# A two-block transformer kernel: first outputs in two parts, LRU off Pool, a narrower causal mask, keys stored once and a new order of tiles in attention

## The chip, the cores and the metric

The kernel runs on one core of a Trainium2 chip. The metric is the device time of one execution in microseconds. The engines are TensorE (PE: matmuls, with PEld for the loading of their weights), VectorE (DVE), ScalarE (ACT), GpSimd (POOL) and SyncE (SP, which issues DMAs). Every DMA is issued from a queue of SP or POOL.

## The reference

The reference computes one token sequence of 1024 tokens and width 1024. Cut to what the change touches:

```python
# first block: gating (4 heads), a state-space branch, cross attention to 256 memory tokens
y = concatenate([y_a * silu(g_a), y_b * silu(g_b), y_x * silu(g_x)], -1)
x = layer_norm(DN_ALPHA * x + y @ w_out, ln_g, ln_b)
# second block, on x normalised again: an LRU branch (conv of 4 taps, gates, a scan over tokens) ...
a = exp(-c * softplus(lam) * r);  h[t] = a * h[t-1] + sqrt(1 - a*a) * (i * x)[t]
# ... and a causal attention with differential heads (two softmaxes of 64-wide heads, subtracted),
# queries and keys RMS-normalised and rotated; then an output product, a mixer over memory, and a MoE
s = where(causal, q @ k.T, -inf);  o = (softmax(s1) - lam * softmax(s2)) @ v
```

All of it is computed in f32 accuracy: an operand is split into a rounded high part and a low part (`split`: ACT copies the high part, DVE subtracts to get the low part), and one product is three matmuls (high x high, low x high, high x low; `mm3`, L174 to L176).

## The kernel before, in words

The program is written as stages that follow each other, and a scheduler fixes a static order of instructions for each engine. In the profile the stages lie so: the first block from 0 to about 338 us, `ln1` (the first block's output product and its layer norm) to 461, `lru` to 705, `attention` to 1460, then the output product, the mixer and the MoE to the end.

**First block to ln1.** The gated outputs of the first block are stored to DRAM tiles `yb[h]` by `store_y` (L527), from SP. In `block1` a lane `left()` handles gating heads 2 and 3, another lane, `attend()`, heads 0 and 1; after a point in the list `LWAT` each a piece of `w_out` is loaded (`self.wo`). `ln1` (L957) works through 8 tiles of 128 tokens: it loads a tile of `yb` (`load`: L1595, split into `yh` and `yl`), multiplies it by `w_out` (`po`, 48 matmuls of 512 columns), adds `x`, normalises (DVE, with POOL for the reciprocal square root of L179 and for the last addition into `x1t`), normalises once more into `xnt`, and transposes (`ptr`, L949) into `xnh` and `xnl`, the operand of everything in the second block.

**LRU.** `lru` (L1036) works through 8 chunks of 128 channels over all 1024 tokens. Each has two projections (`pj`, 48 matmuls of 512 columns each), a convolution on DVE (`xc`), gates (`pg`; `tr` and `ti` on ACT), elementwise work of 128x1024 each on DVE and ACT (`tau`, `ex`, `rn`, `sq`, `q`), and a scan (L1122). In 7 of the 8 chunks two products, `sq*rn` and `ti*sq`, run on POOL. Side work on the memory tokens (`mem2`: `kn`, `kv`, `mh`) lies between.

**Attention.** There are 4 pairs of heads p, each with 16 units (one query tile of 128 tokens, one head half). A unit is: `unit_qk` (L1455), scores `sc` as `qs` x `kh` and `qs` x `kl` in pieces of 256 to 512 key columns, plus one matmul for the causal mask (`ma` x `mb`, L1481, always 256 columns); `unit_mix`, the softmax on DVE and ACT (`st`, `e`); `unit_tr` (L1511), transposes `pt` of the weights, split into `wth` and `wtl`; `unit_pv` (L1523, L1524), `po`; `unit_o`. Between these, generators called `fillers` supply matmuls that do not hang on the softmax: key tiles (project, normalise and rotate in `norm_rope`, transpose), value tiles, query tiles and gate tiles (`pg`, 512 columns). The key side is stored twice in each transposed tile: 4 transposes (L1248) of 128 columns for a key tile of 128 tokens. `need` runs fillers until a query tile exists. After the last unit of a pair come the 8 key and value tiles of the next pair, a key tile and a value tile in turn.

Of the kernel before, what the change touches and what calls it, by code (L numbers as in the profile page):

```python
# [11 lines left out]
F32 = mybir.dt.float32  # L12
# [114 lines left out]
LWAT = (5, 8, 11, 14)  # L127


class Model:  # L130
# [321 lines left out]
    def block1(self):  # L452
# [3 lines left out]
        self.yb = [D.tile([4, 128, 8, 128], F32, name=f"yb{h}") for h in range(2)]  # L456
# [67 lines left out]
        def store_y(k, t0, y, n):  # L524

            i = t0 % 4
            nc.sync.dma_start(out=self.yb[t0 // 4][i:i + n, :, k, :].rearrange("i p t -> p i t"),  # L527
                              in_=y.rearrange("p (i t) -> p i t", i=n))
# [289 lines left out]
        def gating(hp, side, wload, vps, pm_):  # L818
# [25 lines left out]
            def spatial(h, vh, vl):  # L844
                for hh in range(2):
# [17 lines left out]
                    store_y(hd, 4 * h, y, 4)  # L863
                    yield
# [33 lines left out]
        def left():  # L898
# [6 lines left out]
            self.wo = []  # L905
            for n, r in enumerate(gating(1, None, lambda a, b: weights(a, b, "d"), lambda c: (PB, "pb", 2),
                                         (PJ, "pj", 2))):
                yield r
                if n in LWAT:
                    k = len(self.wo)  # L910
                    self.wo.append(self.load_w(LW, A["w_out"][0, k], [128, 2, 512], f"wo0{k}", (W, "wd", 1)))
# [44 lines left out]

    def ln1(self):  # L957
# [4 lines left out]
        with self.pool("lnw1") as LW, self.pool("lny", side="right") as NW, self.pool("ln", side="right") as N, self.pool("lnps", bufs=2, space=PSUM) as PO, \  # L962
                self.pool("lnpt", bufs=2, space=PSUM) as PT:
# [7 lines left out]
            ring = (NW, "raw", 4)  # L971

            def load(i):
                yh = NW.tile([128, 8, 128], F32R, name="yh", tag="yh", bufs=2)
                yl = NW.tile([128, 8, 128], F32R, name="yl", tag="yl", bufs=2)
                eng = nc.gpsimd if i < 2 else nc.sync
                self.load_split(self.yb[i // 4][i % 4], yh, yl, ring, eng)
                return yh, yl

            def load_x(i):  # L980
                xr = N.tile([128, 1024], F32, name="xr", tag="xr", bufs=2)
# [3 lines left out]
            nxt = [load(0), load(1)]  # L985
            nxx = [load_x(0), load_x(1)]
            wo = self.wo + [self.load_w(LW, A["w_out"][1, k], [128, 2, 512], f"wo1{k}", ring) for k in range(4)]
            for i in range(8):
                yh, yl = nxt.pop(0)
                xr = nxx.pop(0)  # L990
                ps = PO.tile([128, 2, 512], F32, name="po", tag="po")
                for n in range(2):
                    for k in range(8):
                        w = wo[4 * n + k // 2]
                        self.mm3(ps[:, n], (yh[:, k], yl[:, k]), (w[0][:, k % 2], w[1][:, k % 2]), k == 0, k == 7)
# [15 lines left out]
                if i < 6:  # L1011
                    nxx.append(load_x(i + 2))
# [8 lines left out]
                self.tt(x1, x1, lb, OP.add, nc.gpsimd)  # L1021
# [7 lines left out]
            finish()  # L1029
            finish()  # L1030
# [1444 lines left out]
```

## Time and profile before

| what | value |
|---|---|
| median of 3 runs | 2524.95 us (2524.49 to 2526.47) |
| the profiled execution: its time, its span | 2524.15 us, 2522.4 us |
| granted TensorE clock, mean | 0.981 |
| busy share of the span | PE 94%, PEld 78%, DVE 71%, ACT 49%, POOL 22% |
| PE busy in the stages: first block / ln1 / lru / attention / rest | 313.5 of 338 / 112.6 of 123 / 229.1 of 244 / 714.5 of 755 / 996.5 of 1062 us |

A profile row of a matmul shows its duration through the pipeline (0.28 us for 256 columns); what it costs on a full PE is the distance from its start to the start of the next. Time that an engine sat idle stands in brackets behind a row of the timeline, with what ended it.

### The profile page before, as it was taken

To read this page: it belongs to the slowest core of one execution; us is meant where nothing else is said; L and a number is where in the kernel's file an instruction comes from. 1 tells how busy PE (TensorE), PEld (TensorE's weight loads), DVE (VectorE), ACT (ScalarE), POOL (GpSimd) and SP (SyncE) were. 2 spreads that over 40 slices of the span, in tenths; PEclk is the share of its full clock that TensorE was granted. 3 is DMA by queue.
4 is the path that set the end of the run, shared out by engine and by line. 5 is a ranking of instruction groups with operands and counts; after the bars stand their busy time and mean duration, and the time that the engine had idled before them with its cause. 6 is when DMAs were issued, how large, how long until landed. Compare 5 with 4: busy or idle time off the path is not lost. (4 is left out here: it accounts for less than half of the span.)

```text
span 2522.4 us, 34498 instructions
## 1 busy us (share of the span) xinstructions
PE 2366.1 (94%) x13016; PEld 1956.4 (78%) x13016; DVE 1786.7 (71%) x3206; ACT 1246.9 (49%) x1850; POOL 546.1 (22%) x377
## 2 busy tenths in 40 slices
PE   8999989989989999899999899999988999988887
PEld 6888868777888898798898778888876777666665
DVE  9667767686876666666666744336658999988887
ACT  5344532553655455455454522124435777766664
POOL 1011114112131021021121100000002333255552
PEclk9999999999999999999999999999988999999999
DMA  6321353322111111111111456532158998999995
GB/s 222 95 76 61 112 200 113 109 70 89 63 60 46 63 46 39 51 51 38 51 51 47 146 198 218 181 137 82 70 217 290 381 372 311 367 335 337 337 334 188
DMA packets 103833, 394.29 MB, mean 156 GB/s; under 512 B 14128, under 2 KB 33072, under 8 KB 79088
## 3 DMA queue, kind: packets, MB, share of 16 engines
q1 hardware_dynamic: 85008, 335.18, 37.6%
q0 software_dynamic: 18656, 56.88, 7.2%
q8 instruction: 104, 1.70, 0.3%
q14 instruction: 65, 0.53, 0.1%
HBM read 339.07 MB, written 61.31 MB: 159 GB/s over the span
## 5 line engine op out<-in xcount | busy, mean ns | idle before, releaser
L166 DVE TENSOR_TENSOR wl<-raw,wh 128x2048 fp32r<-128x2048 f32 (+2 forms) x310 | 580.8, 1887 | 118.3 <-ACT wh L154 118.0
L154 ACT ACTIVATE wh<-raw 128x2048 fp32r<-128x2048 f32 (+2 forms) x310 | 479.7, 1557 | 286.2 <-PE pj L175 83.4
L2238 POOL DMA_INDIRECT out<-y,lsti x32 | 175.2, 5475 | 331.4 <-DVE y L162 281.5
L175 PE MATMUL pg<-wl,xh 128*96 128x512 f32 x512 | 205.4, 401 | 30.2 <-DVE wl L166 30.0
L174 PE MATMUL pj<-wh,xnh 128*128 128x256 f32 x768 | 223.0, 290 | 10.8 <-ACT pc L154 6.0
L175 PE MATMUL pj<-wl,xnh 128*128 128x256 f32 x768 | 218.1, 284 | 0.0
L176 PE MATMUL pj<-wh,xnl 128*128 128x256 f32 x768 | 217.8, 284 | 0.0
L176 PE MATMUL pg<-wh,xl 128*96 128x512 f32 x512 | 201.6, 394 | 0.0
L174 PE MATMUL pg<-wh,xh 128*96 128x512 f32 x512 | 198.2, 395 | 1.0 <-ACT wh L154 1.0
L174 PEld LDWEIGHTS pj<-wh,xnh 128*128 128x128 f32 x768 | 146.0, 190 | 14.3 <-ACT pc L154 8.1
L175 PEld LDWEIGHTS pj<-wl,xnh 128*128 128x128 f32 x768 | 146.2, 190 | 0.0
L176 PEld LDWEIGHTS pj<-wh,xnl 128*128 128x128 f32 x768 | 145.9, 190 | 0.0
L175 PEld LDWEIGHTS pg<-wl,xh 128*96 128x96 f32 x512 | 82.8, 162 | 76.5 <-DVE wl L166 44.6
L179 POOL TENSOR_TENSOR ss<-ss,mhalf 128x4 f32<-128x4 f32 (+1 forms) x68 | 73.0, 1074 | 313.7 <-DVE ss L163 219.3
L154 ACT ACTIVATE e<-sc,st,ss 128x1024 f32<-128x1024 f32 (+7 forms) x128 | 105.7, 829 | 67.3 <-DVE st L158 50.4
L174 PEld LDWEIGHTS pg<-wh,xh 128*96 128x96 f32 x512 | 82.8, 162 | 37.2 <-ACT wh L154 1.4
L174 PE MATMUL pj<-xnh,wh 128*128 128x512 f32 x256 | 103.3, 404 | 5.6 <-ACT wh L154 5.6
L176 PEld LDWEIGHTS pg<-wh,xl 128*96 128x96 f32 x512 | 83.0, 162 | 32.7
L174 PE MATMUL pg<-xnh,wh 128*128 128x512 f32 x256 | 102.9, 402 | 0.0
L175 PE MATMUL pj<-xnl,wh 128*128 128x512 f32 x256 | 102.2, 399 | 0.0
L176 PE MATMUL pg<-xnh,wl 128*128 128x512 f32 x256 | 102.1, 399 | 0.0
L176 PE MATMUL pj<-xnh,wl 128*128 128x512 f32 x256 | 101.9, 399 | 0.0
(998 smaller groups left out, 6480.8 us busy)
## 6 DMA issues: line engine op xcount, KB each, us to landing
raw<-in_w_gu SPq DMA_DIRECT2D x128, 1024.0 KB, 7.3
raw<-in_w_dn SPq DMA_DIRECT2D x64, 1024.0 KB, 9.2
raw<-in_w_out SPq DMA_DIRECT2D x16, 512.0 KB, 4.7
ta<-tg POOLq DMA_DIRECT2D x32, 256.0 KB, 2.6
t<-ta SPq DMA_DIRECT2D x14, 512.0 KB, 4.6
raw<-in_w_ga SPq DMA_DIRECT2D x12, 512.0 KB, 3.8
raw<-in_w_v SPq DMA_DIRECT2D x12, 512.0 KB, 3.4
xraw<-in_xT SPq DMA_DIRECT2D x8, 512.0 KB, 7.6
```

The source lines that it names most:

```text
L154: return self.nc.scalar.activation(out=out, in_=in_, func=func, **kw)
L166: return (eng or self.nc.vector).tensor_tensor(out=out, in0=a, in1=b, op=op)
L174: mm(ps, l[0], r[0], start=start, stop=False)
L175: mm(ps, l[0], r[1], start=False, stop=False)
L176: mm(ps, l[1], r[0], start=False, stop=stop)
L179: self.nc.gpsimd.tensor_tensor(out=out, in0=in_, in1=self.mhalf[:, :w], op=OP.pow)
L2238: return nc.gpsimd.indirect_dma_start(out=self.out, out_offset=bass.IndirectOffsetOnAxis(ap=u["row"], axis=0), in_=u["y"], in_offset=None, ...
```

## The change

It has seven parts.

1. **First outputs in two parts.** `yb[h]` becomes two tensors, one of six columns `YA` (0, 1, 4 to 7) and one of columns 2 and 3. The six-column part of token tile 0 is loaded in `left()` by SP (`y_first`), and `ln1` multiplies it for tiles 0 and 1 ahead of columns 2 and 3. Three pieces of `w_out` are loaded ahead instead of four, the ring of raw buffers in `ln1` has 3 slots instead of 4, and `x` is loaded one tile ahead instead of two.
2. **Last norm's addition.** For token tiles 6 and 7 the addition into `x1t` moves from POOL to DVE.
3. **LRU's first product first.** The first half (512 tokens) of LRU's first projection is written into `ln1`, ahead of the transposes of the last token tile, and copied into `li0`.
4. **LRU off POOL.** `sq*rn` and `ti*sq` run on DVE in all chunks; a small memset moves too; the ring of gate weights "g" has one buffer instead of two.
5. **Mask.** `ma` and `mb` become bf16, and the mask matmul covers 64 columns instead of 256.
6. **Keys once.** `norm_rope` writes a key tile once, so 2 transposes a tile instead of 4; `kk` holds high and low key parts on two halves of the partitions, and `qs` the high and the low part of the queries. A score piece is still two matmuls of the same width.
7. **New order.** The key tiles of the next pair are fillers behind the last gate tiles of this pair; the value tiles of the next pair run within its first unit (`need(vals, p)`). For pair 0 all key tiles come ahead of all value tiles. `tg`, `ot` and `t` share the buffers of `nr`.

```diff
-LWAT = (5, 8, 11, 14)
+LWAT = {5: 0, 8: 2, 11: 3}
+YA = (0, 1, 4, 5, 6, 7)
...
+        self.yb = [[D.tile([4, 128, w, 128], F32, name=f"yb{h}{w}") for w in (6, 2)] for h in range(2)]
...
+                elif n > 8 and not self.y0 and ("gate", 1, 0) in self.made:
+                    self.y0 = self.y_first(YE, 0, (W, "wr", 2))
...
+    def y_first(self, P, i, ring):
+
+        hi = P.tile([128, 6, 128], F32R, name=f"ya{i}h")
+        lo = P.tile([128, 6, 128], F32R, name=f"ya{i}l")
+        return self.load_split(self.yb[i // 4][0][i % 4], hi, lo, ring)
...
-            ring = (NW, "raw", 4)
+            ring = (NW, "raw", 3)
...
+            for k in (4, 6, 7, 1, 5):
+                wo[k] = self.load_w(LW, A["w_out"][k // 4, k % 4], [128, 2, 512], f"wo{k // 4}{k % 4}", ring)
...
+            for i in range(2):
+                product(i, YA)
             for i in range(8):
...
+                product(i, (2, 3) if i < 2 else YA + (2, 3))
...
-                self.tt(x1, x1, lb, OP.add, nc.gpsimd)
+                self.tt(x1, x1, lb, OP.add, nc.vector if i > 5 else nc.gpsimd)
...
             finish()
+
+            ps = P0.tile([128, 512], F32, name="pj", tag="pj")
+            for k in range(8):
+                self.mm3(ps, (self.w0[0][:, k], self.w0[1][:, k]), self.xnc(k, 0), k == 0, k == 7)
+            self.li0 = w0.tile([128, 512], F32, name="li0")
+            self.act(self.li0, ps, AF.Copy)
             finish()
...
-                eng = nc.vector if c == 7 else nc.gpsimd
-                self.tt(sq, sq, rn, OP.mult, eng)
-                self.tt(ti, ti, sq, OP.mult, eng)
+                self.tt(sq, sq, rn, OP.mult)
+                self.tt(ti, ti, sq, OP.mult)
...
-            ma = T.tile([128, 128], F32R, name="ma")
-            mb = T.tile([128, 384], F32R, name="mb")
+            ma = T.tile([128, 128], BF, name="ma")
+            mb = T.tile([128, 64], BF, name="mb")
...
+                w = 1 if is_k else 2
+                d = T1.tile([128, 4, w, 64], F32, name="nr", tag="nr", bufs=3)
...
+                    for m in range(2):
+                        a, b = slice(64 * m, 64 * m + 64), slice(64 - 64 * m, 128 - 64 * m)
+                        g = gcol[a, 1:2]
+                        self.act(kk[0][a, m:4:2, q], pt[a], AF.Copy, scale=g)
+                        self.stt(kk[0][b, m:4:2, q], pt[a], g, kk[0][a, m:4:2, q].bitcast(F32), OP.mult, OP.subtract)
...
+                    if p < 3:
+                        yield "q", p + 1, 0
+                        yield from k_tiles(p + 1, q_tile(p + 1, tiles[0]))
...
-                nc.tensor.matmul(base[:, o:o + n], qs[:, a], kh[:, a, k0:k0 + n], start=True, stop=False)
-                nc.tensor.matmul(base[:, o:o + n], qs[:, a], kl[:, a, k0:k0 + n], start=False, stop=not last)
+                for r in range(2):
+                    nc.tensor.matmul(base[:, o:o + n], qs[:, r, a], kk[:, a, k0:k0 + n], start=r == 0,
+                                     stop=r == 1 and not last)
                 if last:
-                    nc.tensor.matmul(base[:, o + n - 256:o + n], ma, mb[:, 128:384] if i == 0 else mb[:, 0:256],
-                                     start=False, stop=True)
+
+                    end = 128 if i == 0 else o + n
+                    nc.tensor.matmul(base[:, end - 64:end], ma, mb, start=False, stop=True)
...
+                need(vals, p)
```

What the scheduler makes of it is seen in the order of the instructions. On PE, near the last units of pair 0, this is a piece before; `pj` is a filler (a key tile of pair 1, L174 to L176), `pt` transposes the softmax weights of a unit, `sc` are the scores of the next, `po` its products with the values:

```order
L1524 MATMUL po_8357<-V_6649,wtl_8342 128x256
L174 MATMUL pj_8775<-wh_8592,xnh_3988 128x256 [waits Activation_49]
...
L1511 MATMUL pt_8410<-ident_60,e_8325 128x128 [waits DVE_49,PE_49]
L1511 MATMUL pt_8410<-ident_60,e_8325 128x128 x3
L175 MATMUL pj_8775<-wl_8593,xnh_3988 128x256
...
L1478 MATMUL sc_8390<-kh_6647,qs_8386 128x320 [waits DVE_49]
L1479 MATMUL sc_8390<-kl_6648,qs_8386 128x320
L1478 MATMUL sc_8390<-kh_6647,qs_8386 128x320
L1479 MATMUL sc_8390<-kl_6648,qs_8386 128x320
L1481 MATMUL sc_8390<-mb_6618,ma_6617 128x256
```

The same place of the changed program (the names with `kk` are scores, `ma` the mask's weights):

```order
L1608 MATMUL po_8386<-V_7058,wtl_8371 128x256
L1595 MATMUL pt_8439<-ident_60,e_8354 128x128 [waits DVE_49,PE_49]
L1595 MATMUL pt_8439<-ident_60,e_8354 128x128 x3
L1561 MATMUL sc_8419<-kk_6677,qs_8415 128x320 [waits Activation_49]
L1561 MATMUL sc_8427<-kk_6677,qs_8415 128x320
L1561 MATMUL sc_8419<-kk_6677,qs_8415 128x320 [waits DVE_49]
L1561 MATMUL sc_8419<-kk_6677,qs_8415 128x320 x2
L1566 LDWEIGHTS ma_6647
L1566 MATMUL sc_8419<-mb_6648,ma_6647 128x64
```

The 24 matmuls of `pj_8775` (and 24 of `pj_8666`, a little earlier) that lay around the transposes have gone to a later place. The stretch without any filler at the end of pair 0 runs over 48 instructions before (from `sc_8390` on) and over some 95 after; at the ends of pairs 1 and 2 it stays nearly as it was (38 and 48 before, 51 and 51 after). The mask is now an explicit weight load and a matmul of 64 columns.

On DVE, in the LRU's chunk 6, before:

```order
L158 SCALAR_TENSOR_TENSOR rn_6434<-e_6433,ex_6429 128x1024 [waits DVE_49]
L166 TENSOR_TENSOR wl_6630<-raw_6631,wh_6629 128x1024 [waits DMAHW2_49,PE_49,Activation_49]
L158 SCALAR_TENSOR_TENSOR tau_6428<-tau_6428,rn_6434 128x1024 [waits DVE_49]
L158 SCALAR_TENSOR_TENSOR q_6506<-q_6506,pj_6453 128x1024 [waits DMASW4_49,Activation_49]
L166 TENSOR_TENSOR wl_6636<-raw_6637,wh_6635 128x1024 [waits DMAHW3_49,Activation_49]
L158 SCALAR_TENSOR_TENSOR q_6506<-q_6506,pj_6453 128x1024 [waits Activation_49]
L1122 SCALAR_TENSOR_TENSOR e_6443<-tau_6428,ti_6407 128x1024 [waits DVE_49,Pool_49]
```

And after, where the scan (now L1180) no longer waits for POOL:

```order
L159 SCALAR_TENSOR_TENSOR rn_6464<-e_6463,ex_6459 128x1024 [waits DVE_49]
L167 TENSOR_TENSOR wl_6660<-raw_6661,wh_6659 128x1024 [waits DMAHW1_49,PE_49,Activation_49]
L159 SCALAR_TENSOR_TENSOR tau_6458<-tau_6458,rn_6464 128x1024 [waits DVE_49]
L167 TENSOR_TENSOR sq_6467<-sq_6467,rn_6464 128x1024
L159 SCALAR_TENSOR_TENSOR q_6536<-q_6536,pj_6483 128x1024 [waits DMASW5_49,Activation_49]
L167 TENSOR_TENSOR wl_6666<-raw_6667,wh_6665 128x1024 [waits DMAHW2_49,Activation_49]
L167 TENSOR_TENSOR ti_6437<-ti_6437,sq_6467 128x1024 [waits DVE_49]
L167 TENSOR_TENSOR wl_6672<-raw_6673,wh_6671 128x1024 [waits DMAHW3_49,PE_49,Activation_49]
```

`sq` now stands ahead of the first `q` of the next chunk, and `ti` two instructions behind it.

## Rows read from the trace of the kernel before

**Rows 1.** Busy time, LRU: length, PE, PEld, DVE, ACT, POOL, PEclk

```profile
461.00:705.00 244.00, 229.05 (x1048) 188.94 (x1048) 185.63 (x152) 123.42 (x145) 50.69 (x32) 0.95 0.21 73
```

**Rows 2.** PE's timeline, attention, at a mask: start us, duration us

```profile
826.14 0.28 PE L1481 MATMUL sc<-mb,ma 128*128 128x256 f32 x1
826.26 0.28 PE L1524 MATMUL po<-V,wtl 128*128 128x256 f32 x1
...
828.04 0.60 PE L1248 MATMUL pt<-ident,nr 128*128 128x128 f32 x4
828.40 0.48 PE L174 MATMUL pg<-xnh,wh 128*128 128x512 f32 x1
```

**Rows 3.** PE's timeline, first block, 128 columns behind 256

```profile
76.07 0.22 PE L174 MATMUL pst<-xg,Bh 128*128 128x128 f32 x1
76.13 0.27 PE L175 MATMUL pst<-xg,Bh 128*128 128x128 f32 x1
76.24 0.28 PE L176 MATMUL pst<-xg,Bl 128*128 128x128 f32 x1
```

**Rows 4.** PE's timeline, mixer, 16 matmuls of 36 columns

```profile
1742.92 1.87 PE L1982 MATMUL plg<-wrt,hT 128*128 128x36 f32 x16
1744.63 0.36 PE L174 MATMUL sc<-kT,qh 128*128 128x256 f32 x1
1744.83 0.28 PE L175 MATMUL sc<-kT,qh 128*128 128x256 f32 x1
```

**Rows 5.** Groups of PE's instructions, by shape: key/query transposes, mask

```profile
L1248 PE MATMUL pt<-ident,nr 128*128 128x128 f32 x256 | 38.4, 272 | 0.1
L1481 PE MATMUL sc<-mb,ma 128*128 128x256 f32 x128 | 36.4, 285 | 0.0
```

**Rows 6.** What PE waited for, 455 to 750 us: total, times, longest

```profile
PE ptr L949 <- DVE xnt L158: 6.0, 1, 6.0
PE pj L174 <- ACT pc L154: 4.1, 1, 4.1
PE pj L174 <- DVE q L158: 3.7, 1, 3.7
PE pj L174 <- ACT kn L154: 3.0, 1, 3.0
```

**Rows 7.** What PE waited for in the attention, 705 to 1400 us

```profile
PE sc L1478 <- ACT e L154: 10.0, 7, 1.9
PE pt L1511 <- DVE e L158: 7.4, 3, 2.5
```

**Rows 8.** Timelines of POOL and DVE, end of the LRU

```profile
698.08 2.38 POOL L166 TENSOR_TENSOR sq<-sq,rn 128x1024 f32<-128x1024 f32 x1 [9.71 <-ACT wh L154]
700.54 3.26 POOL L166 TENSOR_TENSOR ti<-ti,sq 128x1024 f32<-128x1024 f32 x1
698.11 3.43 DVE L166 TENSOR_TENSOR wl<-raw,wh 128x1024 fp32r<-128x1024 f32 x1 [0.21 <-ACT wh L154]
701.46 3.42 DVE L158 SCALAR_TENSOR_TENSOR tau<-tau,rn 128x1024 f32<-128x1024 f32 x1
705.93 1.22 DVE L166 TENSOR_TENSOR wl<-raw,wh 128x1024 fp32r<-128x1024 f32 x1
```

**Rows 9.** Groups on DVE in the whole LRU, 461 to 705 us

```profile
L166 DVE TENSOR_TENSOR wl<-raw,wh 128x1024 fp32r<-128x1024 f32 x23 | 36.9, 1609 | 29.4 <-ACT wh L154 29.4
L158 DVE SCALAR_TENSOR_TENSOR tau<-tau,rn 128x1024 f32<-128x1024 f32 x7 | 21.4, 3056 | 0.0
```

**Rows 10.** Timelines of POOL, ACT and PE, start of ln1

```profile
331.39 1.18 POOL L1595 DMA_DIRECT2D raw<-yb  x2 [3.06 <-DMA yb<-ya]
337.21 1.06 ACT L154 ACTIVATE yh<-raw 128x1024 fp32r<-128x1024 f32 x1 [1.65 <-DMA raw<-yb]
338.32 0.80 PE L174 MATMUL po<-wo00h,yh 128*128 128x512 f32 x1 [2.73 <-ACT yh L154]
```

**Rows 11.** Timeline of POOL, end of ln1

```profile
453.40 2.39 POOL L166 TENSOR_TENSOR x1t<-x1t,row_ln_b 128x1024 f32<-128x1024 f32 x1 [2.71 <-ACT mh L154]
```

More of the change, by code (lines that the diff above doesn't have):

```diff
@@ new lines, in load_first @@
+            def load_first(i):
+                yh = NW.tile([128, 8, 128], F32R, name="yh", tag="yh", bufs=2)
+                yl = NW.tile([128, 8, 128], F32R, name="yl", tag="yl", bufs=2)
+                y = {}
+                for b, (q, ks) in enumerate(((slice(0, 6), YA), (slice(6, 8), (2, 3)))):
+                    if b == 0 and i == 0 and self.y0:
+                        y.update({k: [z[:, n] for z in self.y0] for n, k in enumerate(YA)})
+                        continue
+                    raw = NW.tile([128, q.stop - q.start, 128], F32, name="raw", tag="raw", bufs=3)
+                    nc.gpsimd.dma_start(out=raw, in_=self.yb[0][b][i])
+                    self.split(yh[:, q], yl[:, q], raw)
+                    y.update({k: (yh[:, q.start + n], yl[:, q.start + n]) for n, k in enumerate(ks)})
+                return y
@@ L980, in load_x @@
             def load_x(i):
-                xr = N.tile([128, 1024], F32, name="xr", tag="xr", bufs=2)
+                xr = N.tile([128, 1024], F32, name="xr", tag="xr", bufs=1)
                 nc.gpsimd.dma_start(out=xr, in_=A["x"][i])
                 return xr
-            nxt = [load(0), load(1)]
-            nxx = [load_x(0), load_x(1)]
-            wo = self.wo + [self.load_w(LW, A["w_out"][1, k], [128, 2, 512], f"wo1{k}", ring) for k in range(4)]
+            nxt = [load_first(0), load_first(1)]
@@ new lines, in ln1, with product @@
+            nxx = [load_x(0)]
+            wo = self.wo
+            for k in (4, 6, 7, 1, 5):
+                wo[k] = self.load_w(LW, A["w_out"][k // 4, k % 4], [128, 2, 512], f"wo{k // 4}{k % 4}", ring)
+            acc = {}
+            def product(i, ks):
+                if i not in acc:
+                    acc[i] = PO.tile([128, 2, 512], F32, name="po", tag="po")
+                for n in range(2):
+                    for k in ks:
+                        w = wo[4 * n + k // 2]
+                        self.mm3(acc[i][:, n], nxt[0][k] if i > 1 else y01[i][k],
+                                 (w[0][:, k % 2], w[1][:, k % 2]), k == 0, k == 3)
@@ L988, in ln1 @@
+            y01 = nxt[:]
+            for i in range(2):
+                product(i, YA)
             for i in range(8):
-                yh, yl = nxt.pop(0)
+                product(i, (2, 3) if i < 2 else YA + (2, 3))
+                nxt.pop(0)
                 xr = nxx.pop(0)
[L991 to L995, printed above, removed]
+                ps = acc.pop(i)
@@ L1059, in proj @@
                 for h in range(2):
-                    for k in range(8):
+                    for k in range(8 if h or late else 0):
                         self.mm3(ps[:, h], (w[0][:, k], w[1][:, k]), self.xnc(k, h), k == 0, k == 7)
@@ L1381, in attention, with need @@
             tail, early = [], []
-            def need(p, i):
+            def need(what, key):
                 alone[0] = True
                 n = 0
-                while (p, i) not in QS:
+                while key not in what:
                     if step() is None:
```

187 lines of the change are left out of this document (103 added, 84 removed).

## The prediction, on record before the run

> **What bounds the kernel now.** I read the busy shares first: PE is busy for 94% of the span, and in each stage for more than 90% of it (the table of times). So what shortens the kernel is either fewer columns through PE or shorter stretches in which PE has nothing to do. In the second place I read what PE waited for, stage by stage. Between 455 and 750 us the long waits end with DVE or with ACT, which itself stands behind DVE [rows 6]; in the attention nearly all waits are for the softmax: 10.0 us for `e` on ACT (a score tile's buffer comes free only when the exponential has read it) and 7.4 us for `e` on DVE, in sum 17.4 us over the three changes from one pair of heads to the next, 5.8 at each [rows 7]. In the third place I read the timeline for what a matmul costs on a full PE, from start to start.
>
> **The mask.** 128 mask matmuls run [rows 5], each 256 columns wide at 0.12 us (826.14 to 826.26 [rows 2]). No row shows one of 64 columns in bf16. The nearest row is a matmul of 128 columns right behind one of 256: its successor starts 0.06 us later, while the ones after it settle at 0.11 [rows 3]; the weights of the next matmul are then still to be loaded. Behind a mask matmul always stands a long one or a run of transposes, so I take 0.06: 128 x (0.12 - 0.06) = 7.7 us less. The bounds: in proportion to the columns it costs 0.03, and 11.5 us are saved; a run of narrow ones, 16 of 36 columns in 1.71 us, costs 0.107 each, and then 0.013 x 128 = 1.7 us are saved; and the first wide matmul after such a run takes 0.20 where 0.12 is usual (1744.63 to 1744.83 [rows 4]). If the mask costs 0.06 and its successor 0.08 more, the sum is 0.14, and 2.6 us are lost. The Trainium skill ("TensorE: Matmul & The Clock Gate", section on LDWEIGHTS) says that loading weights takes their number of columns divided by 1.2 GHz, whatever the matmul behind it; 128 columns would be 107 ns, and by that a mask would hardly get cheaper, 1.7 us in all. The run of 36 columns agrees with it, the single narrow matmul behind a wide one does not.
>
> **Keys once.** Of the 256 transposes on that line [rows 5] half belong to 32 key tiles of 4, half to query tiles. 64 fall away. Four cost 0.36 us (828.04 to 828.40 [rows 2]), so 64 x 0.09 = 5.8 us; at 0.11 each it would be 7. The key parts on ACT and DVE also get smaller; neither is the bound there. The scores keep their widths.
>
> **LRU off POOL.** Fourteen products of 128x1024 go from POOL (2.38 and 3.26 us) to DVE, where such an operation takes 1.22 [rows 8], so DVE gets 17.1 us more. But while POOL runs them, DVE's own operations stretch: `wl` takes 3.43 and ends 1.08 after the first POOL product, `tau` takes 3.42 and ends 1.08 after the second [rows 8]. Over the stage `tau` has a mean of 3.06 and the 23 `wl` one of 1.61 [rows 9]: 7 x 1.84 + 23 x 0.39 = 21.9 us that DVE gets back. DVE gains at least 4.8 us net, out of 185.6 busy in 244 [rows 1]. PE profits only where it waits for DVE: 3.7 us for `q` at the end of the stage, 4.1 for `pc` behind it, 3.0 for `kn` [rows 6]. At `q`, `wl` and `tau` end 2 x 2.2 = 4.4 us earlier, and `sq` stands ahead of it now: 3.2 us earlier. `ti` follows, so that the wait for `pc`, further down the same DVE queue, moves by 2.0 only. With a little for `kn` and for a PE that idles less, I take 4 us less. The bounds are 0 (DVE's new operations stand in front of what PE waits for) and 8 (most of the 10.8 us).
>
> **First outputs in two parts.** PE's first `po` starts at 338.32, 1.1 us after ACT begins `yh` at 337.21, for which it waits 5.8 us after the load was issued at 331.39 [rows 10]. That load waited for the last store of the heads 0 and 1, and the six-column part still holds these heads: it cannot be issued earlier than before. What it gains is a smaller read (384 KB instead of two of 512 KB, and no `w_out` beside it), and a split of 768 columns instead of 1024. I take 1.5 us less. On the other side, one more piece of `w_out` is to be loaded and split within the stage, with a ring of three; PE may catch up with the splits, so the bounds are -4 and +2.
>
> **The ends of ln1.** PE waits 6.0 us for the last `xnt` [rows 6]. POOL's addition takes 2.39 [rows 11], DVE needs 1.22; ACT is busy with other work just then, so I take half the difference, 0.6 us (0 to 2.4). LRU's first product already stands ahead of these transposes in the order of before, so part 3 of the change adds nothing.
>
> **The order in attention.** This is the edit with no sure sign. The filler matmuls stay the same in number; they only move. The order shows that the stretch without a filler at the end of pair 0 grows from 48 instructions to some 95, by spacing from 6.8 us to 13.7 us of PE work; at the other two ends it goes from 5.4 and 6.8 to 7.2. In it each unit's products hang on the softmax of the unit before. Before, such a stretch of 6.8 us brought about 4 us of waiting, of the 5.8 at each change [rows 7]. At the same rate pair 0 costs 4 us more, the others 1 together; DVE has no key tiles to work on meanwhile, which I count as 1 us less. I take +4. What was saved would be that the value tiles cover the first unit of a pair; but before, PE was full there. The bounds: -16, if the new order fills all the waits [rows 7], and +12, if both ends of the longer stretches wait and the clock falls.
>
> **The sum.** -7.7 - 5.8 - 4.0 - 1.5 - 0.6 + 4.0 = -15.6 us, on the profiled execution's 2524.15: 2508.5. The median of the runs shown lies 0.8 above it, so I predict 2509 us.
>
> **The rivals.** *The order pays* (the waits between pairs go): -16 instead of +4 gives about 2489. For it speaks that the tiles of keys no longer compete with the first units; against it the longer stretch without fillers. *The mask pays nothing*: the weights are the price, 0.107 to 0.14 us each. Then the sum is 6 to 10 us less good, 2515 to 2520. By the Trainium skill's rule on LDWEIGHTS cited above it would be the 2515; the trace has rows on either side. *The order costs more*, +12 instead of +4: 2517. *The mask stalls PE* and the kernel gets slower: a bf16 matmul stands between fp32r ones 128 times. If it costs 0.08 us to go in and 0.08 to come out, as the successor of a narrow run does [rows 4], a mask costs 0.22 and 12.8 us are lost instead of 7.7 saved: 2529. It decides from 0.18 us per mask on, where the whole saving of 15.6 us is used up. Speaking against it: in the trace a narrow matmul behind a wide one starts without a gap. *The two parts of the outputs do nothing*, since the last store sets the start: 2511, inside my range.
>
> **How the numbers follow.** The forecast as summed, 2502 to 2514, has a chance of 0.50; the order pays, 0.20; the mask pays nothing, 0.14; the order costs more, 0.09; the mask stalls, 0.07. A measurement of this kernel can tell about 0.2%, 5 us, from no change. Under 2520 lie the first two cases, most of the third, and most of the fourth: faster 0.87. Within 5 us of before lies what is left of these: 0.08. Slower 0.05. The range from 2489 to 2521 leaves out the lower half of "the order pays" and the last case.
>
> **What would show it.** In the profile after, the mask's successor should start about 0.06 us behind it, and PE's busy time in attention should fall by 13 us; `tau` and `wl` in the LRU should have means of about 1.22; the wait for `q` at its end should be under 1 us; the first `po` should start between 335.5 and 338 us; and PE should show waits at the end of pair 0's units of some 8 us where it showed 4. The prediction is wrong if the mask's successor starts later than 0.15 us behind it, if the waits between pairs vanish, or if PE waits more for `w_out` in ln1 than the 1.5 us gained.

## The result and the profile after

The changed kernel takes 2545.28 us (2540.86 to 2547.38, 4 runs), the kernel before 2524.72 beside it: a ratio of 1.0079, interval 1.0061 to 1.0096. It is slower by some 20 us, where 2509 was forecast; the time lies outside the range. Its profiled execution took 2543.79 us, 19.6 above that of before, at a granted clock of 0.973 where it was 0.981.

The first reading of the two traces is where those 19.6 us lie. I took five marks on PE that both programs have (first `po` with `wo00h`, last `ptr` with `xnt`, first scores of the attention, last mask matmul, first `pw` of the mixer) and worked out the distances between their starts:

| stretch, us | before | after | difference |
|---|---|---|---|
| first instruction on PE to first `po` | 330.6 | 330.2 | -0.4 |
| `ln1`: to its last transpose | 124.3 | 129.4 | +5.1 |
| LRU and first keys: to the first scores | 308.9 | 301.7 | -7.2 |
| units of the attention: to the last mask | 659.4 | 663.5 | +4.1 |
| end of the attention, output product: to the mixer | 296.3 | 312.9 | +16.6 |
| rest, to the last matmul | 782.2 | 783.2 | +1.0 |

Windows over the two stretches of the attention split them (length, then the busy time of PE, PEld, DVE, ACT and POOL, granted clock, DMA share, GB/s), before and then after:

```profile
771.60:1431.03 659.43, 631.15 (x4244) 576.61 (x4242) 426.66 (x1085) 330.73 (x684) 98.79 (x112) 0.99 0.15 52
1431.03:1727.28 296.25, 289.19 (x1316) 238.47 (x1315) 122.90 (x161) 79.98 (x115) 21.22 (x31) 0.99 0.51 177
```

```profile
768.90:1432.30 663.40, 626.48 (x4175) 555.29 (x4174) 420.91 (x1108) 332.21 (x705) 98.05 (x111) 0.98 0.14 48
1432.30:1745.20 312.90, 299.21 (x1335) 245.07 (x1334) 125.32 (x160) 81.77 (x118) 21.78 (x32) 0.97 0.51 175
```

PE idles for 36.9 us instead of 28.3 in the units and for 13.7 instead of 7.1 behind them. A part of the +16.6 is work that only moved: 24 matmuls of the first `w_lo` products stood ahead of the last mask and now stand behind it, 5.6 us at 0.23 each. The units have lost these 24 and some 40 transposes (3.9 us at 0.09) and still take 4.1 us longer. So, by this estimate, the units lost some 13 us and the stretch behind them some 11, a stretch for which the prediction has no term at all. PE's busy time, which was to fall by 13 us in the attention, rises by 5.4 over the two.

**The mask.** PE's timeline after, at a mask matmul (start, duration; compare [rows 2]):

```profile
823.23 0.20 PE L1566 MATMUL sc<-mb,ma 128*128 128x64 bf16 x1
823.27 0.36 PE L1608 MATMUL po<-V,wtl 128*128 128x256 f32 x1
823.47 0.28 PE L1607 MATMUL po<-V,wth 128*128 128x256 f32 x1
823.59 0.28 PE L1608 MATMUL po<-V,wtl 128*128 128x256 f32 x1
```

The mask takes 0.04 us now instead of 0.12. But the `po` behind it takes 0.20 (823.27 to 823.47), where the next takes the usual 0.12. The two together cost 0.24 us before and after. So it is behind the other wide matmuls on a full PE: mask and successor take 0.297 and 0.296 us where 384 columns follow, 0.348 and 0.352 where 512 follow (means, before and after). Only where transposes of 128 columns follow, in some 20 places of either trace, does the pair get cheaper, from 0.23 to 0.18 (medians).

**The keys.** The group of key and query transposes has 192 matmuls instead of 256 [rows 5]:

```profile
L1310 PE MATMUL pt<-ident,nr 128*128 128x128 f32 x192 | 32.0, 276 | 2.0 <-DVE nr L167 1.2 <-DVE kk L159 0.8
L1566 PE MATMUL sc<-mb,ma 128*128 128x64 bf16 x128 | 26.7, 208 | 0.0
```

**The LRU.** Groups on DVE after, 465 to 709 us; with [rows 9], the stretched means of 1609 and 3056 ns have become what DVE needs alone:

```profile
L167 DVE TENSOR_TENSOR wl<-raw,wh 128x1024 fp32r<-128x1024 f32 x25 | 30.6, 1223 | 36.0 <-ACT wh L155 36.0
L167 DVE TENSOR_TENSOR sq<-sq,rn 128x1024 f32<-128x1024 f32 x7 | 8.5, 1218 | 0.0
L159 DVE SCALAR_TENSOR_TENSOR tau<-tau,rn 128x1024 f32<-128x1024 f32 x7 | 8.5, 1217 | 0.0
```

What PE waited for from 455 to 750 us (total, times, longest; compare [rows 6]):

```profile
PE pj L175 <- DVE q L159: 7.7, 1, 7.7
PE pj L175 <- ACT wh L155: 6.3, 4, 3.0
PE ptr L957 <- DVE xnt L159: 5.7, 1, 5.7
```

The wait for `q` has grown from 3.7 to 7.7, that for `pc` (4.1) is gone: the waits have changed places.

**The attention.** PE's waits after, 705 to 1400 us, beside [rows 7]:

```profile
PE pt L1595 <- DVE e L159: 8.4, 4, 2.5
PE sc L1561 <- ACT qs L155: 6.6, 9, 1.1
PE sc L1561 <- ACT e L155: 4.0, 4, 1.3
```

`e` on ACT costs 4.0 instead of 10.0, but 6.6 for the queries `qs` are new.

**The end of the attention.** SP's queue of the kernel before shows the loads `t<-ta`, the gate values by which DVE multiplies the results of the first `w_lo` products, among those of the gate parts `gh`:

```profile
1377.89 0.33 SPq L1595 DMA_DIRECT2D raw<-gh  x1
1378.32 26.60 SPq L1576 DMA_DIRECT2D t<-ta  x2
1408.38 2.59 SPq L1595 DMA_DIRECT2D raw<-gh  x2
1412.96 0.32 SPq L1576 DMA_DIRECT2D t<-ta  x1
```

After, the first of them is issued at 1434.69, and the next two at 1451.52:

```profile
1372.58 59.13 SPq L1679 DMA_DIRECT2D raw<-gh  x8
1434.13 0.33 SPq L1679 DMA_DIRECT2D raw<-in_w_lo  x1
1434.69 0.32 SPq L1660 DMA_DIRECT2D t<-ta  x1
...
1451.52 7.82 SPq L1660 DMA_DIRECT2D t<-ta  x2
```

So the products `po<-b00...`, which before filled PE between the last units from 1407.81 on, all stand behind the last scores: of 96 matmuls 24 stood ahead of the last mask and 72 between it and the last product with the values; now it is none and 48, and 48 come later still. A window of 20 us there, before (PE busy, ..., clock, DMA share, GB/s):

```profile
1420.00:1440.00 20.00, 16.83 (x80) 13.31 (x79) 17.43 (x38) 12.48 (x21) 3.57 (x4) 0.91 0.54 180
```

and after:

```profile
1420.00:1440.00 20.00, 11.80 (x47) 9.54 (x46) 17.75 (x38) 13.78 (x23) 2.50 (x2) 0.50 0.53 175
```

PE is busy for 11.8 us instead of 16.8, and the granted clock is 0.50, the lower level of 1.2 GHz, throughout: the softmax of the last units has nothing beside it. The clock is not the main part of the loss, though: e10 below loses nearly as much behind the last mask at 0.83 in this window, and e15 gets a third of it back at 0.50.

**The start of ln1.** SP, ACT and PE after (compare [rows 10]):

```profile
333.70 0.32 SPq L1679 DMA_DIRECT2D raw<-yb  x1
336.89 0.84 ACT L155 ACTIVATE ya0h<-raw 128x768 fp32r<-128x768 f32 x1 [2.92 <-DMA raw<-yb]
337.79 0.80 PE L175 MATMUL po<-wo00h,ya0h 128*128 128x512 f32 x1 [2.71 <-ACT ya0h L155]
```

ACT can start 3.2 us after the issue, not 5.8, but the load is issued 2.3 later; 0.5 us is left of it. (One trace of each is little here: the first `po` starts at 335.8 to 338.5 us in the six traces with the new first outputs, at 338.1 to 342.3 in the fourteen with the old ones, 2.8 earlier on the mean.) Later in the stage a piece of `w_out` that is no longer loaded ahead comes late:

```profile
357.57 1.69 SPq L1679 DMA_DIRECT2D raw<-in_w_out  x2
366.33 1.06 ACT L155 ACTIVATE wo01h<-raw 128x1024 fp32r<-128x1024 f32 x1 [10.31 <-DMA raw<-in_w_out]
367.44 0.74 PE L175 MATMUL po<-wo01h,yh 128*128 128x512 f32 x2 [1.14 <-ACT wo01h L155]
368.70 0.51 PE L176 MATMUL po<-wo01l,yh 128*128 128x512 f32 x1 [0.52 <-DVE wo01l L167]
```

At the end of the stage the addition that POOL did in 2.39 us [rows 11] takes DVE 1.22:

```profile
460.28 1.22 DVE L167 TENSOR_TENSOR x1t<-x1t,row_ln_b 128x1024 f32<-128x1024 f32 x1
```

### The profile page after: what moved, and what is told of

Its sections match the earlier page's. It is cut to its first block, busy times and chain, and to the rows that moved or that the text cites. A ratio compares the mean times of both kernels' runs of the same rounds, so it can differ in the third digit from the quotient of the medians.

```text
span 2541.7 us, 34467 instructions
## 1 busy us (share of the span) xinstructions
PE 2372.7 (93%) x12952; PEld 1941.8 (76%) x12952; DVE 1770.3 (70%) x3266; ACT 1251.6 (49%) x1886; POOL 499.0 (20%) x352
## 5 line engine op out<-in xcount | busy, mean ns | idle before, releaser
L167 DVE TENSOR_TENSOR wl<-raw,wh 128x2048 fp32r<-128x2048 f32 (+3 forms) x310 | 565.4, 1837 | 136.7 <-ACT wh L155 136.4
L155 ACT ACTIVATE wh<-raw 128x2048 fp32r<-128x2048 f32 (+3 forms) x310 | 479.6, 1556 | 296.9 <-PE pj L176 101.5
L176 PE MATMUL pg<-wl,xh 128*96 128x512 f32 x512 | 205.9, 402 | 30.1 <-DVE wl L167 30.0
L176 PE MATMUL pj<-wl,xnh 128*128 128x256 f32 x768 | 218.6, 285 | 0.0
L176 PEld LDWEIGHTS pj<-wl,xnh 128*128 128x128 f32 x768 | 146.7, 191 | 0.0
L176 PEld LDWEIGHTS pg<-wl,xh 128*96 128x96 f32 x512 | 83.0, 162 | 76.7 <-DVE wl L167 44.6
L1561 PE MATMUL sc<-kk,qs 128*128 128x512 f32 (+4 forms) x384 | 100.9, 378 | 14.6 <-ACT qs L155 7.1
L176 PE MATMUL pj<-xnl,wh 128*128 128x512 f32 x256 | 101.6, 397 | 0.0
```

Of the source, the lines that this page charges most:

```text
L155: return self.nc.scalar.activation(out=out, in_=in_, func=func, **kw)
L167: return (eng or self.nc.vector).tensor_tensor(out=out, in0=a, in1=b, op=op)
L176: mm(ps, l[0], r[1], start=False, stop=False)
L1561: nc.tensor.matmul(base[:, o:o + n], qs[:, r, a], kk[:, a, k0:k0 + n], start=r == 0, stop=r == 1 and not last)
```

## The experiments

Theories changed on the way. The first was the new order of tiles (theory 1), the second the buffers that `tg`, `ot` and `nr` share, the third (theory 3) one pair in that ring: `t` waits for `ot`. All times are medians; the kernel before ran on the same chips at 2526.05 to 2527.53.

**e1: the old order in the changed kernel.**

```diff
-                    if p < 3:
-                        yield "q", p + 1, 0
-                        yield from k_tiles(p + 1, q_tile(p + 1, tiles[0]))
...
+                    yield from k_tiles(p)
+                    gate_w(4 * p)
```

> The changed kernel with the order of tiles in the attention as it was before (key and value tiles in turn after a pair's last unit, the old release of query tiles), everything else changed. Theory 1 (the new order costs most of the loss: waits within the units and at the end of attention): 2545 - 24 = about 2521 us, and the b0 products again between the last units. Rival (the mask in bf16 and the two-part queries slow the units, whatever the order): 2540 us or more, with PE still waiting for qs.

Measured: 2545.51, ratio 1.0066 (1.0054 to 1.0078). The old order alone gives nothing back. Theory 1 in its plain form fell; e18 shows that this run could not see the order's price.

**e2: the first outputs and `ln1` as before, in the changed kernel** (parts 1, 2 and 3 of the change undone).

> The changed kernel with the first outputs, ln1 and LRU's first product as before; LRU off POOL and the attention as changed. Theory 1 (ln1 loses 5 us to w_out pieces that come late, and nothing else hangs on it): about 2540 us, with the last ptr 4 to 5 us earlier. Rival (the part in ln1 is hidden, or it moves what comes behind): within 2 us of 2545, or under 2535.

Measured: 2538.16, ratio 1.0038 (1.0025 to 1.0051): 7.1 us less than the changed kernel.

**e3: only the LRU off POOL, in the kernel before.**

```diff
-                self.tt(sq, sq, rn, OP.mult, eng)
-                self.tt(ti, ti, sq, OP.mult, eng)
+                self.tt(sq, sq, rn, OP.mult)
+                self.tt(ti, ti, sq, OP.mult)
```

> The kernel before with only sq*rn and ti*sq of the LRU moved from POOL to DVE. Theory 1 (DVE gets more time back than it is given; the wait for pc behind the LRU goes): 7 us less than before, about 2518 us. The prediction's own term: 4 us less, 2521. Rival (DVE becomes the bound of the stage): 2525 us or more, with PE waiting longer for q.

Measured: 2523.00, ratio 0.9981 (0.9972 to 0.9991): 4.0 us less, the prediction's term.

**e4 and e8: only the mask, in the kernel before**, once in bf16, once as 64 columns of the old type. Both also set `ma` and `mb` on DVE instead of POOL.

```diff
-            ma = T.tile([128, 128], F32R, name="ma")
-            mb = T.tile([128, 384], F32R, name="mb")
+            ma = T.tile([128, 128], BF, name="ma")
+            mb = T.tile([128, 64], BF, name="mb")
...
+                    nc.tensor.matmul(base[:, end - 64:end], ma, mb, start=False, stop=True)
```

> The kernel before with only the mask changed: bf16, 64 columns. Theory 1 (the mask matmul costs 0.04 us, but its successor starts 0.08 us later than usual): within 1 us of before, 2524 to 2526. The prediction's term: 7.7 us less, 2517. Rival (the bf16 matmul stalls PE on both sides): 2530 us or more.

> The kernel before with a mask of 64 columns that stays fp32r. If the late successor of the bf16 mask (0.08 us) comes from the change of type, here it starts without delay, and the kernel is 5 us faster than with the bf16 mask of 64 columns, about 2517 us. If it comes from the loading of the next weights behind a short matmul, the successor is as late as there and the time the same, 2522 us. If a narrow fp32r matmul runs at a lower rate, the mask takes over 0.06 us and its successor nothing extra.

Measured: bf16 2522.07, ratio 0.9982 (0.9973 to 0.9991); the old type 2525.60, ratio 0.9995 (0.9986 to 1.0004). PE's timeline of e8 at a mask:

```profile
822.38 0.19 PE L1483 MATMUL sc<-mb,ma 128*128 128x64 f32 x1
822.41 0.36 PE L1525 MATMUL po<-V,wtl 128*128 128x256 f32 x1
822.61 0.28 PE L1524 MATMUL po<-V,wth 128*128 128x256 f32 x1
```

0.03 for the mask and 0.20 for its successor: the same late successor without any change of type. So it is the short matmul, not bf16 between fp32r, that makes it late. Neither time is one that was expected, and why e4 gains 5 us and e8 only 1 is not settled: the pair of matmuls costs the same in both to 0.01 us, and the intervals of the two ratios overlap. The granted clock goes with it: it is 0.979 to 0.981 in the runs of e4 and 0.976 to 0.981 in those of e8, whose two runs at 0.980 and above took 2522.25 and 2522.50.

**e5, e9, e10: only the shared ring, in the kernel before.** The loads `t` were in nr's ring already. e5 puts `tg` and `ot` into nr's ring of three, e9 makes it a ring of five, e10 puts only `ot` there.

```diff
-            ot = T.tile([128, 512], F32, name="ot", tag="ot", bufs=1)
+            ot = self.at1.tile([128, 512], F32, name="ot", tag="nr", bufs=3)
```

> The kernel before with only tg and ot moved into the ring of three buffers of nr. Theory 2 (the shared ring holds the gate tiles and the transposed query tiles back, so that the static order has stretches of 11 us without a filler at the end of every pair): 10 to 18 us more than before, with PE waiting for the softmax at the end of each pair and a low clock at the end of attention. Rival (the queries in two parts and the keys stored once do it): no change, within 2 us of before.

> The kernel before with tg and ot in the ring of nr, as in the run with the ring alone, but with five buffers in the ring: as many as nr, tg and ot had together. Theory 2a (on the chip, tiles wait for one of three buffers): the loss goes, 2525 to 2530 us. Theory 2b (the sharing changes the static order, in which PE then stands without fillers; the buffers themselves are no limit): as with three, 2544 to 2550 us, with the same waits for the softmax at the end of each pair.

> The kernel before with ot alone in the ring of nr; tg keeps its own buffer. If ot alone does the harm: 2540 us or more. If it takes both: within 3 us of before, 2524 to 2529 us (its order of PE shows stretches without fillers as long as before's).

Measured: e5 2547.88, ratio 1.0084 (1.0070 to 1.0098); e9 2547.07, 1.0081 (1.0067 to 1.0095); e10 2544.71, 1.0078 (1.0064 to 1.0092). One line, without any other part of the change, costs the kernel before 18.4 us; two more buffers don't help, and `tg` need not be there too. The end in SP's queue of e10 is that of the changed kernel:

```profile
1380.86 45.77 SPq L1596 DMA_DIRECT2D raw<-gh  x7
...
1441.81 15.97 SPq L1577 DMA_DIRECT2D t<-ta  x2
```

and its stretch from the last mask to the mixer takes 311.0 us, before 296.3.

**e6 and e7: LRU, mask and keys once, with the old order of tiles** (and one buffer for `kk`), e6 with the shared ring, e7 with `tg` and `ot` in buffers of their own. Between the two:

```diff
-                t = T1.tile([128, 512], F32, name="tg", tag="nr", bufs=3)
+                t = T.tile([128, 512], F32, name="tg", tag="tg", bufs=1)
...
-            ot = self.at1.tile([128, 512], F32, name="ot", tag="nr", bufs=3)
+            ot = T.tile([128, 512], F32, name="ot", tag="ot", bufs=1)
```

> The kernel before with LRU off POOL, the mask in bf16, keys once with two-part queries, the old order of tiles, one buffer for kk, and tg and ot in the ring of nr. Theory 2: 2535 to 2542 us. Rival: the same.

> As the run with the shared ring, but tg and ot in buffers of their own: two lines differ. Theory 2: the loss is gone and the gains of LRU (4), mask (4) and keys (5) add up: 2510 to 2515 us. Rival (keys once and two-part queries): as with the shared ring, 2535 us or more.

Measured: e6 2535.17, ratio 1.0035 (1.0022 to 1.0049); e7 2509.73, ratio 0.9937 (0.9924 to 0.9951). Two lines are worth 25 us, and e7 is faster than both kernels of this study.

**e11 and e12: e7 with the new first outputs, `ln1` and first LRU product (e11), and e7 with only the addition of tiles 6 and 7 on DVE (e12).**

```diff
-                self.tt(x1, x1, lb, OP.add, nc.gpsimd)
+                self.tt(x1, x1, lb, OP.add, nc.vector if i > 5 else nc.gpsimd)
```

> The fast variant (LRU off POOL, mask, keys once, old order, buffers of their own) with the changed first outputs, ln1, x1 addition and LRU's first product added. Theory (ln1 loses by pieces of w_out that come late): 4 to 6 us slower than without, 2514 to 2516 us. The prediction's terms for these parts: 2 us faster than without, 2508.

> The fast variant with only the last norm's addition of tiles 6 and 7 moved to DVE. The prediction's term: 0.6 us faster, 0 to 2.4, so 2508 to 2510. Rival (DVE's queue makes the last xnt later): 2511 or more.

Measured: e11 2514.16, ratio 0.9954 (0.9940 to 0.9968), 4.4 us more than e7; e12 2510.86, 0.9935 (0.9921 to 0.9949), no difference from e7.

**e13: e10, with `t` in a buffer of its own.**

```diff
-                t = T.tile([128, 512], F32, name="t", tag="nr", bufs=3)
+                t = T.tile([128, 512], F32, name="t", tag="te", bufs=1)
```

> The kernel before with ot in the ring of nr, as in e10 (2544.71, ratio 1.0078), but with the loads t of the first w_lo products in a buffer of their own (it takes the room that ot gave up). Theory 3 (what costs is that t shares a ring with ot, which is stored last, so that the w_lo products cannot run between the last units): the order on PE holds 22 us of these products between the last units and the last products with the values, as before, where e10's holds 11, so 2526 +-4, ratio 0.999 to 1.001, and the clock between 1420 and 1440 us does not fall to 0.5. Rival (the queries and keys in nr wait for ot, whatever t does): 2545 as in e10. A time near 2535 would give each of them half.

Measured: 2532.27, ratio 1.0021 (1.0012 to 1.0030). 12.4 of e10's 18.4 us come back, and the stretch from the last mask to the mixer is 297.5 us, 1.2 from that of before. All 72 matmuls of the `w_lo` products stand between the last mask and the last product with the values again, where e10 has 24. The 6 us that remain lie ahead of it (the units take 668.6 us, in e10 665.6, before 659.4; the profiled execution is the slowest of e13, 3.7 above its median). So theory 3 accounts for two thirds. That the last third is the rival, other tiles of the ring that wait for `ot`, is argued, not shown.

**e14 and e16: the changed kernel with `ot` in another ring**, that of the squares (tag `e11`, which has nothing to do with the run e11); e16 also with `ln1` as before.

```diff
-            ot = self.at1.tile([128, 512], F32, name="ot", tag="nr", bufs=3)
+            ot = T.tile([128, 4, 128], F32, name="ot", tag="e11", bufs=1).rearrange("p a b -> p (a b)")
```

> The changed kernel with ot in the ring of osq (e11, one buffer) instead of nr's; tg and t stay in nr's ring. The order on PE then holds 21 us of w_lo products between the last units and the last products with the values, where the changed kernel's holds 11. Theory 3: the 17 us that the changed kernel loses between the last scores and the mixer come back, 2528 +-4, ratio 0.999 to 1.003 to the kernel before. Rival (the new order of tiles or the new layout of keys makes the end dear by itself): it stays at 2542 to 2546. ot waits for the squares in its ring, which may cost 1 or 2 us at the end of each head.

> e14 with the first outputs, ln1 and the first product of the LRU as before too: what is left of the change is LRU, mask, keys once, new order, and tg in nr's ring. If the parts add up, e14 less 5 to 7 us (e2 gave 7, e11 4.5): 2521 to 2523, ratio 0.998 to 0.999. e7, with the old order of tiles and own buffers, took 2509.73; the 12 us between the two would be the price of the new order, which e1 could not show, since there the shared ring hid it. If this run comes to 2510 to 2514, the new order costs nothing.

Measured: e14 2557.62, ratio 1.0123 (1.0107 to 1.0139); e16 2550.91, 1.0094 (1.0080 to 1.0109). Both expectations missed. The stretch to the mixer did come back, in part (306.2 us, and from the last transposes of `ot` on 267.4, as before), but the units now take 686.7 us instead of 663.5. PE's waits in e14, 705 to 1380 us, say for what (`pc` is ACT's copy of a projected tile, `kk` the finished keys):

```profile
PE pj L175 <- ACT pc L155: 20.2, 12, 5.1
PE pt L1310 <- DVE kk L159: 8.1, 3, 2.7
```

ACT's timeline and then PE's, at the change to pair 1:

```profile
907.43 0.69 ACT L155 ACTIVATE ot<-pt,sub 128x512 f32<-128x512 f32 x1 [6.12 <-PE pt L1633]
```

```profile
917.68 0.58 PE L175 MATMUL pj<-wh,xnh 128*128 128x256 f32 x1 [5.08 <-ACT pc L155]
```

ACT stands still for 6.1 us in front of `ot`, whose transposes PE does behind key tiles; the work on the key tiles (`pc`, `nq`, `kk`) piles up behind it, and PE, which has only key tiles to do here, then waits for ACT.

**e15: the changed kernel with `t` in the ring of the queries.**

```diff
-                t = T.tile([128, 512], F32, name="t", tag="nr", bufs=3)
+                t = self.at[0].tile([128, 512], F32, name="t", tag="qs", bufs=3)
```

> The changed kernel with the loads t of the first w_lo products in the ring of the queries qs, not in nr's. The loads are then issued among those of the gate parts, as before, and wait for no ot; but the order on PE is, but for one row, that of the changed kernel: 11 us of w_lo products behind the last scores, none ahead of them. This parts the two halves of theory 3. If the wait of the loads is the cost, 2528; if the order on PE that came of it (no filler between the last units) is the cost, the time stays at 2540 to 2546. I expect the order: 2542.

Measured: 2537.70, ratio 1.0040 (1.0026 to 1.0054): 7.6 us come back although the order on PE is nearly the same. The last mask to the mixer takes 307.1 us instead of 312.9, with the clock still at 0.50 between 1420 and 1440 us. The wait of the loads and the place of the products on PE each have a part in the loss; 2542, all order, was off.

**e17 and e18: the changed kernel with `tg` and `ot` apart**, in room taken from the query ring; e18 also with `ln1` as before.

```diff
-            QB = 3
+            QB = 2
...
-            ot = self.at1.tile([128, 512], F32, name="ot", tag="nr", bufs=3)
+            ot = T.tile([128, 512], F32, name="ot", tag="ot", bufs=1)
```

> The changed kernel with buffers of their own for tg and ot, as in e7; t stays with nr as it was before. The room comes from the ring of queries qs, two buffers instead of three. (In e14 the end of the attention had come back, 267.4 us instead of 284.2 from the last transposes of ot to the mixer, but there ot stood ahead of the key tiles on ACT and PE waited 20 us for pc.) Theory 3: own buffers give what they gave between e6 and e7, 25 us: 2520 +-5, ratio 0.996 to 1.000. Rival (the new order of tiles needs its room elsewhere, and its longer stretches without fillers cost by themselves): 2530 to 2540, with the units between 770 and 1430 us no shorter than in the changed kernel. The smaller ring of queries may cost a few us of either.

> e17 with the first outputs, ln1 and the first product of the LRU as before. Against e17: 5 to 7 us less, the price of the new first outputs, as e2, e11 and e16 gave (7.3, 4.5 and 6.7). Against e7 (2509.73, the same with the old order of tiles and three query buffers): what is more than 2510 is the price of the new order with its smaller ring of queries. If the order is as good as the old one, 2510 to 2515; by the prediction's own term (+4), 2514; if the longer stretches without fillers cost what I took for their bound (+12), 2522.

Measured: e17 2540.70, ratio 1.0059 (1.0047 to 1.0071); e18 2535.13, 1.0033 (1.0020 to 1.0046). The rival held: without the shared ring the new order still costs. The clock between 1420 and 1440 us is 1.00 in e18, and the last mask to the mixer takes 300.6 us; but the units take 671.9 us, where e7's take 655.0. PE's waits from 705 to 1400 us in e18:

```profile
PE pj L174 <- ACT pc L154: 16.2, 9, 3.4
PE pt L1252 <- DVE kk L158: 8.1, 3, 2.7
PE pt L1537 <- DVE e L158: 5.3, 3, 2.5
```

and in e7:

```profile
PE pt L1518 <- DVE e L158: 7.4, 3, 2.5
PE sc L1484 <- ACT e L154: 5.1, 7, 1.3
```

The 24.3 us for `pc` and `kk` don't exist in e7. They are the price by place too: 32 matmuls of the `w_lo` products (7.4 us at 0.23) stand behind the last mask in e18 and ahead of it in e7, so that of the differences of 16.9 us in the units and 8.7 behind them some 24 belong to the units. PE's timeline of e18 shows them at the change to pair 1, where key tiles follow each other with no unit between:

```profile
910.70 0.58 PE L174 MATMUL pj<-wh,xnh 128*128 128x256 f32 x1 [3.35 <-ACT pc L154]
...
917.32 0.39 PE L174 MATMUL pj<-wh,xnh 128*128 128x256 f32 x1 [1.62 <-ACT pc L154]
...
923.57 0.63 PE L1252 MATMUL pt<-ident,nr 128*128 128x128 f32 x4 [2.70 <-DVE kk L158]
```

## Why the prediction was wrong

Four runs with the LRU, the mask and the keys changed and `ln1` as before show it:

| | old order | new order |
|---|---|---|
| `tg`, `ot` in buffers of their own | e7: 2509.73 | e18: 2535.13 |
| `tg`, `ot` in nr's ring | e6: 2535.17 | e2: 2538.16 |

Either edit alone costs 25 us; both together cost 28.4 (by the ratios to the kernel before on the same chips 24.8 and 24.3, together 25.5). That is why undoing one of them in the changed kernel showed little (e1 nothing, e17 4.6). The ring's 25 us in the old order are a clean comparison, of two lines. The new order's are not quite: there is one buffer of keys in the left column and two in the right, and two buffers of queries in e18, three elsewhere; what these cost alone was not run. Two things limit it. e16, with the new order and three query buffers, shows the same waits, 20.9 us for `pc` and 8.1 for `kk` (its `ot` waits elsewhere, too). And e1 and e6 differ only in parts 1 to 3, priced at 4.4 to 7.1 below, and in the second buffer of keys, and lie 10.3 us apart, so that this buffer costs a few us at most.

**The step that failed** is the term for the order in attention: +4 us, with bounds of -16 and +12, where the measured price of part 7 is +28.4. Two things were missing from it. The prediction counted what a stretch without fillers costs the *units*, by the waits for the softmax [rows 7]; those did not grow, they fell, from 17.4 us to 12.4 in the changed kernel and 6.9 in e18, though 6.6 for `qs` came in beside them in the changed kernel. But the fillers that were taken away stand elsewhere, in a block of key tiles, and in e18 PE waits there for the work on the key tiles themselves: where 1 us less was counted because DVE has no key tiles meanwhile, it waits 16.2 us for ACT and 8.1 for DVE. And the last sentence of part 7, that `tg`, `ot` and `t` share nr's buffers, got no price at all. What it needed stands in the code: `ot` is the last tile of a head to be finished, `t` the first of the next product. Which of the two losses a kernel shows depends on the static order: in the changed kernel, with its ring, the waits for `pc` and `kk` are only 3.4 us, and the loss lies at the end (+16.6 us, of which 5.6 moved there) and in the units; in e14 and e18 it lies at the changes of pairs. How the ring costs the units their part was not traced.

**First outputs in two parts**: -1.5 forecast, and -0.6 for the end of `ln1`; measured +7.1 (changed kernel against e2), +4.4 (e11 against e7), +6.7 (e14 against e16) and +5.6 (e17 against e18). The sign of the whole was wrong, not that of the start: it came at 337.79, inside the forecast of 335.5 to 338, and over all traces 2.8 us earlier on the mean. What was mis-sized is the cost of one more piece of `w_out` in the stage, and what comes behind had no term. The piece `wo01`, now loaded inside the stage behind stores on SP, comes late (PE waits 1.1 us for its high and 0.5 for its low part), and when PE starts again at 356.59 after a wait for `wo10l`, which is as long as before, eight matmuls of 512 columns lie 0.43 us apart, where those of before lie 0.23 apart: 1.6 us. These make up 3.3 us. Over all traces `ln1` takes 3.7 us more with the new outputs (means of 128.5 and 124.7), more than the earlier start gives. Behind it PE's wait for `q` at the end of the LRU is 7.7 us in all six traces with the new outputs and 5.5 in the six with the old ones and parts 4 to 6: 2.2 more, not explained. The rest is not traced. My bound of +2 was too low. The addition on DVE gave nothing that can be seen in the time (e12: 1.1 more than e7), though the wait for `xnt`, 5.7 in the changed kernel, is 4.4 to 4.5 in the five other traces with all three parts, where it was 6.0.

**The mask**: -7.7 forecast. The rival *the mask pays nothing* was right about the row: the mask and what it adds to its successor come to 0.24 - 0.12 = 0.12 us, inside that rival's 0.107 to 0.14 and just what the wide mask cost. The row that I chose by, 128 columns behind 256 [rows 3], has no late successor; the one that I set aside, a late successor of 0.20 behind a narrow run [rows 4], was the right one. The condition on record looked at the wrong place: the successor starts 0.04 us behind the mask, and the cost sits one instruction further on. The Trainium skill ("TensorE: Matmul & The Clock Gate", section on LDWEIGHTS) gives the time of a weight load by the columns of the weights alone; the estimate worked out from that in the prediction, 1.7 us saved in all, comes near to what the rows show, nothing behind wide matmuls.

**LRU off POOL**: -4 forecast, -4.0 measured (e3); the means of `wl` and `tau` came to 1.22 us as forecast. But the wait for `q` did not fall under 1 us: it is 1.9 in e3 and 7.7 in the changed kernel.

**Keys once**: no run has it alone. With LRU and mask it gives e7's 16.8 us, where these three terms summed to 17.5. If e3's 4.0 and e4's 4.9 add up in it, 7.9 are left for the keys, 5.8 forecast; with e8's 0.9 for the mask it would be 11.9. That they add up was not shown.

**The sum**: -16.8 for the three, +28.4 for part 7, +7.1 for `ln1`: +18.7, measured 20.6. That it comes out confirms nothing: the three are differences along one row of kernels, before to e7 to e2 to the changed one, and what is missing is the 1.8 us between the kernel before on two chips.

## What to carry to other kernels

When tiles are put into one ring, look for the one that is finished last and the one that is wanted first after it: the ring makes the second wait for the first, a static schedule then moves everything that hangs on it, and more buffers need not cure it. Fillers that are moved must be costed at both places: where they are missing, and where they now stand in a block with nothing beside them. And when two edits hide each other's price, undoing one proves nothing; take both out and put each back alone.

## What the runs showed of the hardware that was not expected

The cost of a narrow matmul shows in its successor. 64 columns take 0.03 us from start to start in the old type and 0.04 in bf16, and the 256-column matmul behind them takes 0.20, where 0.12 is usual; 256 columns for the mask take 0.12 and leave the successor at 0.12.

A wait of the same length is paid differently. PE waits 1.7 us for `wo10l` in both kernels; behind it the matmuls of 512 columns run at half pace for 3.5 us in the changed kernel (356.59 to 360.06) and at full pace in the kernel before. It is the granted clock: 0.52 there, about its lower level of 1.2 GHz, and 1.00 before (PE busy first, clock third from the end; after, then before):

```profile
356.59:360.06 3.47, 3.47 (x9) 2.73 (x10) 2.22 (x2) 0.00 (x0) 0.00 (x0) 0.52 1.07 284
```

```profile
358.02:361.38 3.36, 3.36 (x14) 2.75 (x15) 3.35 (x3) 0.37 (x1) 1.11 (x2) 1.00 1.01 185
```

In the 6 us ahead of it the changed kernel idles once more, 0.69 us for `mx`.
